# Both parts of the activation as one 512-column moving operand in the streamed products of a two-layer decoder trunk, one output per accumulator bank, weights split 1024 columns at a time

## The chip, the cores and the metric

The kernel runs on one core of one Trainium2 chip. The metric is the device time of one launch in microseconds (us). Three runs of the kernel before took 921.65, 922.49 and 922.83 us; the median is 922.49 us.

## The reference, cut to what matters

Sequence 256, width 1024, float32. Layer 0 mixes tokens by attention in three dilated groups, layer 1 by an mLSTM block. After each mixer come a squared-ReLU MLP and a gated embedding.

```
x += dilated_attention(rms_norm(x) ...) @ w_o          # layer 0, w_qkv 1024 x 9216
x += mlstm(rms_norm(x) @ w_up ...) @ w_down            # layer 1, w_up 1024 x 4096
x += square(relu(rms_norm(x) @ w1)) @ w2               # each layer, hidden 4096
x += sigmoid(rms_norm(x) @ w_gate) * (p @ w_proj)      # each layer
```

Features lie on the 128 partitions, tokens (256) along the free axis, so a product reads the weights as the stationary operand (128x128) and the activation as the moving one (256 columns per block of 128 features).

## The kernel before, in words

**Two parts.** Weights and activations are float32 and are multiplied as float32r. Each is split in two, a high part (ScalarE copy into float32r, L176 for weights, L298 for activations) and a low part (VectorE, value minus high part, L177 and L299). A product is hi*hi + hi*lo + lo*hi: three matmuls.

**The stream of weights.** All weights lie in units of 128 x 2048 (`UC`), 138 in all, loaded by SyncE four units ahead (`LD`). A unit is four slots of 512 columns; a slot is four weight tiles of 128x128. `open_slot` issues the split of slots up to `lead` ahead (7 in the qkv stage, 11 later), each into one of 12 buffers of 512 columns (`HU`) for either part. A split waits for the buffer, so for the matmuls that read it 12 slots before. The splits have a low priority (`BACK`): the scheduler puts them behind more urgent work in the queues.

**Stages, in order:** qkv with the attention between it (36 units; here the weights are the moving operand, 512 columns, L499 to L501), proj0 (1 unit), wo in two parts woA (k 0 to 5, 3 units) and woB (k 6 and 7, 1 unit), w1_0 (16), w2_0 (16), gate0 (4), xm (8), z0 to z3 (8) with the mLSTM core between them, wd0 (4), proj1 (1), wd1 (4), w1_1 (16), w2_1 (16), gate1 (4). From proj0 on, every product goes through `stream` (L318): per weight tile three matmuls of 256 columns, L331 (hi weights, high activation), L332 (hi weights, low activation), L333 (lo weights, high activation). Without the two proj stages that is 100 units, 1600 tiles.

**Accumulators.** `psa` has 3 buffers of one PSUM bank. Mostly a bank holds a pair of outputs o (2 x 256 columns); w2 and the end of woB, gate and wd1 have one output per bank. When all k of a block are done, `done` empties the bank: ReLU and square in w1 (L646 to L650), times the norm factor in w2 (L658), gate (L669), xm (L774) and z (L929), an addition to x in wo and wd (L623).

**Norm factors.** `rstd_rows` sums squares 2 slots after a stage's start (`SA`) and spreads the factor over the partitions 6 slots after it (`SB`): small VectorE operations, two scalings of the identity (L291), two matmuls (L293), a copy (L294, tile rb). In gate and xm the emptying of the first banks needs that factor and is put off by 3 slots (`DF`).

The order on each engine is set by a list scheduler from program order and priorities; queues are in order, so whoever waits holds up all behind it.

```
mm(acc[:, q], wh, h, start=first, stop=False, ...)   # L331
mm(acc[:, q], wh, l, start=False, stop=False, ...)   # L332
mm(acc[:, q], wl, h, start=False, stop=last, ...)    # L333
```

Of the kernel before, what the change touches and what calls it, by code (L numbers as in the profile page):

```python
# [14 lines left out]
ALU = mybir.AluOpType  # L15
# [14 lines left out]
HU = 512  # L30
# [9 lines left out]
def _blocks(no, ks, singles=0):  # L40

    n = no - singles
    os = [(o, o + 1) for o in range(0, n, 2)] + [(o,) for o in range(n, no)]
    return [(b, list(ks)) for b in os]

# [94 lines left out]
def _build(ctx, tc, nc, a):  # L140
# [17 lines left out]

    raw, hi, lo = {}, {}, {}
# [23 lines left out]
    CH = 512  # L183
    WARM = 9
    BACK = 100

    LQ, LS, LD = 7, 11, 4
    fill = {}
    clock = [0]
    ahead = [7]  # L190
# [6 lines left out]
    DF = 3  # L197
# [51 lines left out]
    hA = [base.tile([P, KT, S], F32R, name=f"h{n}") for n in "hl"]  # L249
# [68 lines left out]
    def stream(blocks, rhs, done, defer=0):  # L318

        i = 0  # L320
        for os, ks in blocks:
            n = len(os)
            acc = psa.tile([P, n, S], F32, name="acc")
            for k in ks:
                for q, o in enumerate(os):
# [3 lines left out]
                    h, l = rhs(k)  # L329
                    first, last = k == ks[0] and q == 0, k == ks[-1]  # L330
# [3 lines left out]
                    if last and q == n - 1:  # L334
                        if defer and i < 16:
                            at(clock[0] + defer, done, os, acc)
                        else:
                            done(os, acc)
# [4 lines left out]
    def from_h(h):  # L343
        return lambda k: (h[0][:, k], h[1][:, k])
# [79 lines left out]
    oT = [atp.tile([P, KT, S], F32R, name=f"oT{n}") for n in "hl"]  # L424
# [58 lines left out]
    def qkv_block(qt, what, g):  # L483
# [591 lines left out]
```

## Time and profile before

| | |
|---|---|
| median of three runs | 922.49 us |
| the profiled execution | 921.63 us, its span 919.9 us |
| TensorE (PE) busy | 904.3 us, 98% |
| VectorE (DVE) busy | 659.7 us, 72% |
| ScalarE (ACT) busy | 569.5 us, 62% |
| GpSimd (POOL) busy | 41.5 us, 5% |
| DMA | 150.23 MB, 163 GB/s mean |
| mean granted TensorE clock | 0.997 |

Busy time is the time in which an engine had at least one instruction in flight; matmuls and operations overlap their neighbours, so a pitch (start to start of neighbours that wait for nothing) is shorter than a duration. PEld is the weight load. A wait is put down to the instruction that released it. In the window view a matmul that is cut by an edge counts in both windows.

### The profile page before, as it was taken

The numbers are of one execution on the slowest core, as the hardware profiler recorded it, in microseconds if no ns is written. First come the engines' busy times: TensorE is split into PE (matmuls) and PEld (weight loads), VectorE is DVE, ScalarE is ACT, GpSimd is POOL, SyncE is SP. The second block draws the span as 40 slices with busy tenths as digits, with TensorE's granted clock in tenths as the row PEclk, the third lists the DMA queues.
The fourth block names the chain that finished last, engine by engine and source line by source line (L and its number), as shares of the span: only waits on it lengthen the run. The fifth ranks groups of instructions, "written<-read, shape, count | busy, mean of one in ns | idle before, by whom it ended". The sixth has DMA issues, their size and how long they took to land.

```text
span 919.9 us, 17609 instructions
## 1 busy us (share of the span) xinstructions
PE 904.3 (98%) x6924; PEld 844.3 (92%) x6924; DVE 659.7 (72%) x1409; ACT 569.5 (62%) x1055; POOL 41.5 (5%) x77
## 2 busy tenths in 40 slices
PE   8799999999999999999999999999999999999997
PEld 6687787877889999999999899999999999999997
DVE  6966877857866866665667987568898666656664
ACT  7567576575585766654446686668866666644442
POOL 0400000000000000000000542000000000000000
PEclk9999999999999999999999999999999999999999
DMA  8744443544443555555555433343265555555521
GB/s 302 281 142 160 156 144 133 178 136 145 154 161 105 178 185 183 184 183 184 183 184 183 157 129 104 127 138 98 87 220 204 184 183 184 184 183 182 184 94 46
DMA packets 23122, 150.23 MB, mean 163 GB/s; under 512 B 2560, under 2 KB 3200, under 8 KB 5632
## 3 DMA queue, kind: packets, MB, share of 16 engines
q1 hardware_dynamic: 23040, 149.12, 47.1%
q8 instruction: 54, 0.88, 0.4%
q14 instruction: 28, 0.23, 0.1%
HBM read 148.06 MB, written 1.05 MB: 162 GB/s over the span
## 4 chain that ended last, share of the span: by engine, by line
PE 92%; DVE 6%; ACT 1%; issue 1%; DMA 0%; SPq 0%; ACTq 0%
PE acc L331 21%; PE acc L332 21%; PE acc L333 21%; PE acc L499 6%; PE acc L501 6%; PE acc L500 6%; DVE lo L177 2%; PE tp L451 1%; PE tp L552 1%; PE sm L570 1%; PE sc L527 1%; PE tp L741 1%; PE tp L751 1%; PE sc L882 1%; PE sc L759 1%; PE sc L533 1%
## 5 line engine op out<-in xcount | busy, mean ns | idle before, releaser
L177 DVE TENSOR_TENSOR lo<-raw,hi 128x512 fp32r<-128x512 f32 x552 | 375.6, 691 | 176.7 <-ACT hi L176 175.3
L176 ACT ACTIVATE hi<-raw 128x512 fp32r<-128x512 f32 x552 | 339.2, 628 | 227.1 <-PE acc L332 204.4
L331 PE MATMUL acc<-hh,hi 128*128 128x256 f32 x640 | 184.0, 288 | 0.3 <-ACT hh L298 0.2
L332 PE MATMUL acc<-hl,hi 128*128 128x256 f32 x640 | 181.5, 284 | 0.1
L333 PE MATMUL acc<-hh,lo 128*128 128x256 f32 x640 | 181.4, 283 | 0.0
L331 PE MATMUL acc<-hidh,hi 128*128 128x256 f32 x512 | 144.9, 283 | 0.0
L332 PE MATMUL acc<-hidl,hi 128*128 128x256 f32 x512 | 144.9, 283 | 0.0
L333 PE MATMUL acc<-hidh,lo 128*128 128x256 f32 x512 | 144.9, 283 | 0.0
L331 PEld LDWEIGHTS acc<-hh,hi 128*128 128x128 f32 x640 | 122.4, 191 | 1.6 <-issue 0.7
L332 PEld LDWEIGHTS acc<-hl,hi 128*128 128x128 f32 x640 | 122.5, 191 | 0.7 <-DVE hl L299 0.5
L333 PEld LDWEIGHTS acc<-hh,lo 128*128 128x128 f32 x640 | 122.4, 191 | 0.0
L499 PE MATMUL acc<-hi,hh 128*128 128x512 f32 x264 | 109.6, 416 | 0.0
L500 PE MATMUL acc<-lo,hh 128*128 128x512 f32 x264 | 104.1, 394 | 0.8 <-DVE lo L177 0.8
L501 PE MATMUL acc<-hi,hl 128*128 128x512 f32 x264 | 104.2, 395 | 0.0
L331 PEld LDWEIGHTS acc<-hidh,hi 128*128 128x128 f32 x512 | 98.3, 192 | 0.0
L332 PEld LDWEIGHTS acc<-hidl,hi 128*128 128x128 f32 x512 | 98.3, 192 | 0.0
L333 PEld LDWEIGHTS acc<-hidh,lo 128*128 128x128 f32 x512 | 98.3, 192 | 0.0
L331 PE MATMUL acc<-hBh,hi 128*128 128x256 f32 x320 | 90.9, 284 | 0.0
L332 PE MATMUL acc<-hBl,hi 128*128 128x256 f32 x320 | 90.7, 283 | 0.0
L333 PE MATMUL acc<-hBh,lo 128*128 128x256 f32 x320 | 90.6, 283 | 0.0
L331 PEld LDWEIGHTS acc<-hBh,hi 128*128 128x128 f32 x320 | 61.4, 192 | 0.3 <-issue 0.3
L332 PEld LDWEIGHTS acc<-hBl,hi 128*128 128x128 f32 x320 | 61.4, 192 | 0.0
(258 smaller groups left out, 1384.3 us busy)
## 6 DMA issues: line engine op xcount, KB each, us to landing
raw<-w SPq DMA_DIRECT2D x136, 1024.0 KB, 4.9
raw<-w SPq DMA_DIRECT2D x8, 256.0 KB, 6.8
x<-x SPq DMA_DIRECT2D x4, 256.0 KB, 5.4
pj<-rep SPq DMA_DIRECT2D x1, 896.0 KB, 6.9
out<-u SPq DMA_DIRECT2D x3, 256.0 KB, 2.4
pT<-p SPq DMA_DIRECT2D x2, 256.0 KB, 4.0
nd<-nd SPq DMA_DIRECT2D x1, 384.0 KB, 6.2
out<-u SPq DMA_DIRECT2D x2, 128.0 KB, 1.9
```

Of the source, the lines that this page charges most:

```text
L176: act(hi[n][:, d], raw[u][:, s], AF.Copy)
L177: dve.tensor_tensor(lo[n][:, d], raw[u][:, s], hi[n][:, d], op=ALU.subtract)
L331: mm(acc[:, q], wh, h, start=first, stop=False, skip_group_check=n > 1)
L332: mm(acc[:, q], wh, l, start=False, stop=False, skip_group_check=n > 1)
L333: mm(acc[:, q], wl, h, start=False, stop=last, skip_group_check=n > 1)
L451: nc.tensor.transpose(ps[:, pair, b * P:(b + 1) * P], n[:, b, ty * 256 + pair * P:ty * 256 + (pair + 1) * P], ident)
L499: mm(accs[b], hh, wh, start=(k == 0), stop=False)
L500: mm(accs[b], hh, wl, start=False, stop=False)
L501: mm(accs[b], hl, wh, start=False, stop=(k == 7))
L527: mm(ps[:, 0:256], q[r, pair, tb], k[r, pair], start=first, stop=last)
L533: mm(ps[64 * e:64 * e + 64, 256 + 64 * n:320 + 64 * n], QT[qt, g][0][r, pair, t4], KTt[qt, g][0][r, pair, t4], start=True, stop=True)
L552: nc.tensor.transpose(psf[:, k * P:(k + 1) * P], pe[:, k * P:(k + 1) * P], ident)
```

## The change

Each activation is one tile with both parts behind each other ([P, 2, k, 256]), and a matmul with the hi weights takes both parts of one k as one moving operand of 2 x 256 columns (the two runs lie KT x 256 or, in the MLP, 32 x 256 elements apart). Its result fills a whole bank: one half has hi*hi, the other hi*lo; the lo*hi matmul adds into the first half. So a tile has two matmuls, 512 and 256 columns, and a bank holds one output. Whoever empties it adds the halves: `whole`, a ScalarE copy of one half and a VectorE addition of the other, or two additions to x. The proj stages keep the old form (`stream_pairs`). A split covers 1024 columns, two slots, into one of 6 buffers; the leads are 6 and 10. In gate and xm the bank is emptied at once and the rest of the work waits for the factor (`late`). A stage begins with two outputs side by side, the others follow one by one (w2 and z: all one by one). The input of proj shares its tiles with others (tags).

```diff
-HU = 512
+HU = 1024
-def _blocks(no, ks, singles=0):
-    n = no - singles
-    os = [(o, o + 1) for o in range(0, n, 2)] + [(o,) for o in range(n, no)]
+def _blocks(no, ks, first=2):
+    os = [tuple(range(first))] + [(o,) for o in range(first, no)]
...
-        with tc.high_priority(offset=-(BACK if back is None else back)):
-            act(hi[n][:, d], raw[u][:, s], AF.Copy)
-            dve.tensor_tensor(lo[n][:, d], raw[u][:, s], hi[n][:, d], op=ALU.subtract)
+        s = slice(c * 512, (c + n) * 512)
+        d = slice(c * 512 % HU, c * 512 % HU + n * 512)
+        with tc.high_priority(offset=-back):
+            act(hi[t][:, d], raw[u][:, s], AF.Copy)
+            dve.tensor_tensor(lo[t][:, d], raw[u][:, s], hi[t][:, d], op=ALU.subtract)
+    def parts(p, name, *shape, **k):
+        t = p.tile([P, 2, *shape], F32R, name=name, **k)
+        return [t, t[:, 0], t[:, 1]]
-    LQ, LS, LD = 7, 11, 4
+    LQ, LS, LD = 6, 10, 4
-        while ahead[0] < clock[0] + lead[0]:
-            ahead[0] += 1
+        while ahead[0] + 2 <= clock[0] + lead[0]:
+            ahead[0] += 2
             split(*divmod(ahead[0], 4))
...
-    def stream(blocks, rhs, done, defer=0):
+    def stream(blocks, h, done):
-            acc = psa.tile([P, n, S], F32, name="acc")
+            accs = [psa.tile([P, 2, S], F32, name="acc") for _ in os]
...
-                    mm(acc[:, q], wh, h, start=first, stop=False, skip_group_check=n > 1)
-                    mm(acc[:, q], wh, l, start=False, stop=False, skip_group_check=n > 1)
-                    mm(acc[:, q], wl, h, start=False, stop=last, skip_group_check=n > 1)
+                    mm(acc.rearrange("p a b -> p (a b)"), wh, h[0][:, :, k], start=first, stop=False, skip_group_check=True)
+                    mm(acc[:, 0], wl, h[1][:, k], start=False, stop=last, skip_group_check=True)
+                    if last:
+                        done(o, acc)
...
+    def late(t0, f, *args):
+        if clock[0] > t0 + SB:
+            f(*args)
+        else:
+            at(t0 + SB, f, *args)
+    def whole(out, acc):
+        act(out, acc[:, 1], AF.Copy)
+        dve.tensor_tensor(out, out, acc[:, 0], op=ALU.add)
...
-    prep, ph = proj(0, atp, ("n0", "n1", "sqh"))
+    prep, ph = proj(0, atp, ("sqh", "nqk"))
...
-            dve.tensor_tensor(x[:, span(os)], x[:, span(os)], acc, op=ALU.add)
+            for n in range(2):
+                dve.tensor_tensor(x[:, o], x[:, o], acc[:, n], op=ALU.add)
...
-            act(u, acc, AF.Relu)
-            dve.tensor_tensor(s, u, u, op=ALU.mult)
-            act(hid[0][:, span(os)], u, AF.Square)
-            dve.tensor_tensor(hid[1][:, span(os)], s, hid[0][:, span(os)], op=ALU.subtract)
+            whole(u[:, o % 2], acc)
+            if o % 2:
+                dve.scalar_tensor_tensor(s, u, 0.0, u, op0=ALU.max, op1=ALU.mult)
+                act(hid[1][:, o - 1:o + 1], s, AF.Copy)
+                dve.tensor_tensor(hid[2][:, o - 1:o + 1], s, hid[1][:, o - 1:o + 1], op=ALU.subtract)
...
-            dve.tensor_tensor(t, acc[:, 0], r2, op=ALU.mult)
+            whole(t, acc)
+            dve.tensor_tensor(t, t, r2, op=ALU.mult)
...
+        def rest(o, t):
+            dve.tensor_tensor(t, t, rb, op=ALU.mult)
+            act(g, t, AF.Sigmoid)
+            dve.tensor_tensor(t, g, pj[:, o], op=ALU.mult)
+            finish(o, t)
+        def done(o, acc):
+            t = tmp.tile([P, S], F32, name="gt", bufs=3)
+            whole(t, acc)
+            late(t0, rest, o, t)
-        stream(B_GATE, from_h(h2), done, DF)
+        stream(B_GATE, h2, done)
...
-        dve.tensor_tensor(xm, acc, urb[0][:, None, :].to_broadcast([P, 2, S]), op=ALU.mult)
+        whole(xm[:, o % 2], acc)
+        late(xm0, xm_rest, o - 1, xm)
+    def xm_rest(o, xm):
+        dve.tensor_tensor(xm, xm, urb[0][:, None, :].to_broadcast([P, 2, S]), op=ALU.mult)
...
-            dve.tensor_tensor(t, acc, urb[0][:, None, :].to_broadcast([P, 2, S]), op=ALU.mult)
-            act(sz[:, span(os)], t, AF.Silu)
+            whole(t[:, o % 2], acc)
+            if o % 2:
+                dve.tensor_tensor(t, t, urb[0][:, None, :].to_broadcast([P, 2, S]), op=ALU.mult)
+                act(sz[:, o - 1:o + 1], t, AF.Silu)
```

TensorE in w1_0, before (acc is the bank, hh and hl the parts of the activation, hi and lo those of the weights):

```order
L331 MATMUL acc<-hh,hi 128x256
L332 MATMUL acc<-hl,hi 128x256
L333 MATMUL acc<-hh,lo 128x256
L331 MATMUL acc<-hh,hi 128x256
L332 MATMUL acc<-hl,hi 128x256
L333 MATMUL acc<-hh,lo 128x256
```

And now (h is the activation with both parts):

```order
L338 MATMUL acc<-h,hi 128x512
L339 MATMUL acc<-h,lo 128x256
L338 MATMUL acc<-h,hi 128x512
L339 MATMUL acc<-h,lo 128x256
L338 MATMUL acc<-h,hi 128x512
L339 MATMUL acc<-h,lo 128x256
```

Three matmuls and three weight loads of a tile have become two of each.

VectorE in gate0 from the first operation that needs the factor rb, before (u is the emptied pair of outputs, s its sigmoid, xn the next layer's input, hl and hh its parts):

```order
L669 TENSOR_TENSOR u_6020<-acc_5877,rb_5876 128x512
L669 TENSOR_TENSOR u_6049<-acc_5949,rb_5876 128x512
L177 TENSOR_TENSOR lo_6065<-raw_5882,hi_6064 128x512
L672 TENSOR_TENSOR u_6020<-s_6022,pj_198 128x512
L672 TENSOR_TENSOR u_6049<-s_6051,pj_198 128x512
L697 TENSOR_TENSOR xn_5870<-x_82,u_6020 128x4x4x16 x2
L697 TENSOR_TENSOR xn_5870<-x_82,u_6049 128x4x4x16
L299 SCALAR_TENSOR_TENSOR hl_116<-xn_5870,prm_83,hh_115 128x256 x2
L697 TENSOR_TENSOR xn_5870<-x_82,u_6049 128x4x4x16
L177 TENSOR_TENSOR lo_6083<-raw_5954,hi_6082 128x512
```

And now (gt is one emptied output; L376 is the addition of the halves):

```order
L704 TENSOR_TENSOR gt_4852<-gt_4852,rb_4804 128x256
L704 TENSOR_TENSOR gt_4857<-gt_4857,rb_4804 128x256
L704 TENSOR_TENSOR gt_4883<-gt_4883,rb_4804 128x256
L707 TENSOR_TENSOR gt_4852<-s_4920,pj_189 128x256
L707 TENSOR_TENSOR gt_4857<-s_4927,pj_189 128x256
L738 TENSOR_TENSOR xn_4799<-x_82,gt_4852 128x4x4x16
L738 TENSOR_TENSOR xn_4799<-x_82,gt_4857 128x4x4x16
L182 TENSOR_TENSOR lo_4998<-raw_4865,hi_4997 128x1024
L306 SCALAR_TENSOR_TENSOR h_115<-xn_4799,prm_83,h_115 128x256 x2
L707 TENSOR_TENSOR gt_4883<-s_4936,pj_189 128x256
L376 TENSOR_TENSOR gt_4950<-gt_4950,acc_4886 128x256
L738 TENSOR_TENSOR xn_4799<-x_82,gt_4883 128x4x4x16
```

The chain works on one output at a time; the emptying of the fourth output's bank (acc_4886) stands inside it, behind a split of 1024 columns.

ScalarE at the end of gate1, before:

```order
L294 ACTIVATE rb_11025<-sm_11077 128x256
L671 ACT_TABLE_LOAD
L671 ACTIVATE s_11159<-u_11157 128x512
L671 ACTIVATE s_11178<-u_11176 128x512
L671 ACTIVATE s_11234<-u_11232 128x512
L671 ACTIVATE s_11266<-u_11264 128x256
L671 ACTIVATE s_11298<-u_11296 128x256
```

And now, its last ten:

```order
L375 ACTIVATE gt_8856<-acc_8801 128x256
L375 ACTIVATE gt_8882<-acc_8865 128x256
L375 ACTIVATE gt_8908<-acc_8891 128x256
L706 ACTIVATE s_8860<-gt_8856 128x256
L706 ACTIVATE s_8886<-gt_8882 128x256
L706 ACTIVATE s_8912<-gt_8908 128x256
L375 ACTIVATE gt_8934<-acc_8917 128x256
L375 ACTIVATE gt_8960<-acc_8943 128x256
L706 ACTIVATE s_8938<-gt_8934 128x256
L706 ACTIVATE s_8964<-gt_8960 128x256
```

The copy of the last output's half (acc_8943) stands ahead of the last two sigmoids.

## Rows read from the trace of the kernel before

**Rows 1.** The page: busy time, and the chain that ended last, by engine
```profile
PE 904.3 (98%) x6924; PEld 844.3 (92%) x6924; DVE 659.7 (72%) x1409; ACT 569.5 (62%) x1055; POOL 41.5 (5%) x77
...
PE 92%; DVE 6%; ACT 1%; issue 1%; DMA 0%; SPq 0%; ACTq 0%
```

**Rows 2.** Windows: start:end, length, busy and instructions per engine, PEclk, DMA
```profile
20.00:40.00 20.00, 19.11 (x91) 15.06 (x89) 19.69 (x51) 13.26 (x26) 4.84 (x7) 1.00 0.72 263
40.00:60.00 20.00, 14.92 (x65) 12.17 (x66) 14.24 (x34) 8.86 (x18) 7.82 (x15) 0.91 0.56 191
...
300.00:320.00 20.00, 19.90 (x167) 19.73 (x166) 18.05 (x37) 14.60 (x29) 0.00 (x0) 1.00 0.55 197
340.00:360.00 20.00, 20.00 (x169) 20.00 (x169) 13.70 (x22) 11.87 (x20) 0.00 (x0) 1.00 0.60 202
500.00:520.00 20.00, 19.65 (x160) 19.05 (x160) 18.71 (x38) 16.49 (x31) 4.58 (x3) 1.00 0.34 116
520.00:540.00 20.00, 18.74 (x141) 17.64 (x141) 19.37 (x44) 14.08 (x26) 13.07 (x24) 1.00 0.49 164
...
640.00:660.00 20.00, 20.00 (x157) 19.11 (x156) 16.52 (x50) 14.92 (x26) 0.00 (x0) 1.00 0.38 134
660.00:680.00 20.00, 20.00 (x166) 19.85 (x166) 19.38 (x47) 14.39 (x29) 0.00 (x0) 1.00 0.48 170
```

**Rows 3.** Timeline of TensorE in qkv: start, duration, line, tiles
```profile
62.13 0.39 PE L499 MATMUL acc<-hi,hh 128*128 128x512 f32 x1
...
66.89 0.39 PE L499 MATMUL acc<-hi,hh 128*128 128x512 f32 x1
```

**Rows 4.** Timeline of TensorE in w1_0
```profile
344.87 0.28 PE L332 MATMUL acc<-hl,hi 128*128 128x256 f32 x1
...
349.91 0.28 PE L332 MATMUL acc<-hl,hi 128*128 128x256 f32 x1
```

**Rows 5.** Groups by line and shape: busy us, mean ns, idle before
```profile
L177 DVE TENSOR_TENSOR lo<-raw,hi 128x512 fp32r<-128x512 f32 x552 | 375.6, 691 | 176.7 <-ACT hi L176 175.3
L658 DVE TENSOR_TENSOR u<-acc,rb 128x256 f32<-128x256 f32 x16 | 6.8, 425 | 2.4 <-PE acc L333 0.4
```

**Rows 6.** Timeline of VectorE in w1_0: five splits in a row
```profile
311.35 3.09 DVE L177 TENSOR_TENSOR lo<-raw,hi 128x512 fp32r<-128x512 f32 x5
```

**Rows 7.** Timeline of VectorE at the end of w2_0
```profile
487.97 0.43 DVE L659 TENSOR_TENSOR x<-x,u 128x256 f32<-128x256 f32 x1
488.31 0.68 DVE L177 TENSOR_TENSOR lo<-raw,hi 128x512 fp32r<-128x512 f32 x1
```

**Rows 8.** Who waited for whom: total us, times, longest
```profile
PE tp L451 <- DVE nqk L443: 5.2, 2, 5.0
...
PE sm L293 <- DVE dg L291: 1.3, 1, 1.3
```

**Rows 9.** Timeline of TensorE after its longest wait, in qkv
```profile
44.89 0.45 PE L451 MATMUL tp<-ident,nqk 128*128 128x128 f32 x1 [5.02 <-DVE nqk L443]
...
45.56 0.63 PE L500 MATMUL acc<-lo,hh 128*128 128x512 f32 x1
45.98 0.63 PE L501 MATMUL acc<-hi,hl 128*128 128x512 f32 x1
```

**Rows 10.** Timeline in gate0, all engines: the factor rb
```profile
498.51 0.37 ACT L294 ACTIVATE rb<-sm 128x256 f32<-128x256 f32 x1
```

**Rows 11.** Timeline of VectorE at the start of xm
```profile
517.30 0.52 DVE L299 SCALAR_TENSOR_TENSOR hl<-xn,prm,hh 128x256 fp32r<-128x256 f32 x1
```

**Rows 12.** Timeline at the end, after the last matmul
```profile
915.23 0.42 DVE L669 TENSOR_TENSOR u<-acc,rb 128x256 f32<-128x256 f32 x1 [1.02 <-PE acc L333]
915.75 0.42 ACT L671 ACTIVATE s<-u 128x256 f32<-128x256 f32 x1 [2.46 <-DVE u L669]
916.20 0.43 DVE L672 TENSOR_TENSOR u<-s,pj 128x256 f32<-128x256 f32 x1 [0.54 <-ACT s L671]
916.66 0.42 DVE L978 TENSOR_TENSOR u<-xn,u 128x256 f32<-128x256 f32 x1
```

More of the change, by code (lines that the diff above doesn't have):

```diff
@@ L29, with _pairs @@
 UC = 2048
-HU = 512
+HU = 1024
 SC = 384
 PI = np.array([16 * c + 4 * b + a for a in range(4) for b in range(4) for c in range(16)])
-def _blocks(no, ks, singles=0):
-    n = no - singles
-    os = [(o, o + 1) for o in range(0, n, 2)] + [(o,) for o in range(n, no)]
+def _blocks(no, ks, first=2):
+    os = [tuple(range(first))] + [(o,) for o in range(first, no)]
     return [(b, list(ks)) for b in os]
+def _pairs(no, ks):
+    return [((o, o + 1), list(ks)) for o in range(0, no, 2)]
 def _qkv():
@@ L247, in pr @@
         return prm[:, o:o + w]
-    hA = [base.tile([P, KT, S], F32R, name=f"h{n}") for n in "hl"]
+    hA = parts(base, "h", KT, S)
     sqp = pool("sq", 2)
@@ L328, in stream @@
                     wh, wl = weights(u, (i % 16) * P, P)
[L329 to L338 removed]
+                    acc, first, last = accs[q], k == ks[0], k == ks[-1]
+                    mm(acc.rearrange("p a b -> p (a b)"), wh, h[0][:, :, k], start=first, stop=False, skip_group_check=True)
+                    mm(acc[:, 0], wl, h[1][:, k], start=False, stop=last, skip_group_check=True)
+                    if last:
+                        done(o, acc)
                     if i % 4 == 3:
@@ L341, in stream, with stream_pairs @@
                     i += 1
-    def from_h(h):
-        return lambda k: (h[0][:, k], h[1][:, k])
+    def stream_pairs(blocks, h, done):
+        i = 0
+        for os, ks in blocks:
+            acc = psa.tile([P, 2, S], F32, name="acc")
+            for k in ks:
+                for q, o in enumerate(os):
+                    if i % 4 == 0:
+                        u, c = open_slot()
+                    wh, wl = weights(u, (i % 16) * P, P)
+                    first, last = k == ks[0] and q == 0, k == ks[-1]
+                    mm(acc[:, q], wh, h[1][:, k], start=first, stop=False, skip_group_check=True)
+                    mm(acc[:, q], wh, h[2][:, k], start=False, stop=False, skip_group_check=True)
+                    mm(acc[:, q], wl, h[1][:, k], start=False, stop=last, skip_group_check=True)
+                    if last and q == 1:
+                        done(os, acc)
+                    if i % 4 == 3:
+                        close_slot()
+                    i += 1
+    def late(t0, f, *args):
[6 more added lines that the diff above has]
+        dve.tensor_tensor(out, out, acc[:, 0], op=ALU.add)
     actx = ExitStack()
@@ L422, in _build @@
     at(44, small_products)
-    oT = [atp.tile([P, KT, S], F32R, name=f"oT{n}") for n in "hl"]
+    oT = parts(atp, "oT", KT, S)
     QT, KTt, VT = {}, {}, {}
@@ L602, in proj @@
         nc.sync.dma_start(ptile, a["p"][layer])
-        ph = [p.tile([P, 2, S], F32R, name=f"pT{n}", tag=tags[n]) for n in (1, 2)]
+        ph = parts(p, "pTp", 2, S, tag=tags[1])
         def prep():
-            act(ph[0], ptile, AF.Copy)
-            dve.tensor_tensor(ph[1], ptile, ph[0], op=ALU.subtract)
+            act(ph[1], ptile, AF.Copy)
+            dve.tensor_tensor(ph[2], ptile, ph[1], op=ALU.subtract)
         return prep, ph
-    prep, ph = proj(0, atp, ("n0", "n1", "sqh"))
+    prep, ph = proj(0, atp, ("sqh", "nqk"))
     prep()
@@ L676, in _build @@
     mctx = ExitStack()
     mp = pool("mlp0", c=mctx)
-    hid = [mp.tile([P, 32, S], F32R, name=f"hid{n}") for n in "hl"]
+    hid = parts(mp, "hid", 32, S)
     hgp = pool("hG", c=xctx0, side="right")
-    hG = [hgp.tile([P, KT, S], F32R, name=f"hG{n}") for n in "hl"]
+    hG = parts(hgp, "hG", KT, S)
     gst = Stats()
@@ L687, in _build @@
     xn = xp1.tile([P, KT, S], F32, name="xn")
-    hB = [xp1.tile([P, KT, S], F32R, name=f"hB{n}") for n in "hl"]
+    hB = parts(xp1, "hB", KT, S)
     mctx = ExitStack()
@@ L876, in memory @@
         nums = []
+        sq = zp.tile([P, 2, 512], F32, name="nsq")
         ss = None
@@ L972, in _build, with finish1 @@
     mp = pool("mlp1", c=mctx)
-    hid = [mp.tile([P, 32, S], F32R, name=f"hid{n}") for n in "hl"]
+    hid = parts(mp, "hid", 32, S)
     gst = Stats()
     mlp(1, x, hB, mst, hid, mp, hA, "gP1", gst)
-    def finish1(os, t):
-        dve.tensor_tensor(t, x[:, span(os)], t, op=ALU.add)
-        nc.sync.dma_start(a["out"][:, span(os)], t)
+    def finish1(o, t):
+        dve.tensor_tensor(t, x[:, o], t, op=ALU.add)
+        nc.sync.dma_start(a["out"][:, o], t)
     gate(1, hA, gst, mp, finish1)
```

148 lines of the change are left out of this document (73 added, 75 removed).

## The prediction

> **What bounds the kernel now.** I read the page first. TensorE is busy for 98% of the span and 92% of the chain that ended last is its own work [rows 1]. An edit gains what it takes from TensorE's queue and loses every wait that it puts into it; work on VectorE and ScalarE counts only through such waits. Next come the windows [rows 2]: in w1_0 (340:360) TensorE has no idle time and does 169 matmuls in 20 us at full clock. VectorE has 6 us to spare there, but only 2.0 in woB (300:320), 1.3 where gate0 goes into xm (500:520), and 0.6 in xm's first part (520:540) and in wd0 (660:680). The list of waits holds one long wait of TensorE, 5.0 us, and one of 1.3 us for a factor's diagonals [rows 8].
>
> Last, the timeline for the two pitches. From 62.13 to 66.89 lie 21 matmuls of 512 columns: 4.76/21 = 226.7 ns each [rows 3]. From 344.87 to 349.91 lie 42 of 256: 5.04/42 = 120.0 ns [rows 4]. At the higher level (2.4 GHz) the columns themselves take 213.3 and 106.7 ns, so a matmul pays 13.3 ns beside its columns at either width.
>
> **Term 1, the matmuls.** A tile had three matmuls, 3 x 120.0 = 360.0 ns. It will have one of 512 and one of 256: 226.7 + 120.0 = 346.7 ns. Columns and results are the same; one fixed cost of 13.3 ns goes. 100 units of 16 tiles give 1600 x 13.3 ns = 21.3 us. All of it lies on TensorE, thus on the path: **-21.3 us**. What the rows don't show is a moving operand in two runs, far apart: those of both rows are contiguous. Bounds: the jump is free (-21.3), or a second run pays what a matmul pays, 13.3 ns (0). I take free: the fixed part is the same at both widths, so it goes with the instruction and not with the columns read.
>
> The Trainium skill's page "TensorE: Matmul & The Clock Gate", section "Wait — 56ns, not 53.3ns?", gives about 2.5 ns beside the columns, 215.7 ns at 512. By it 1600 x 2.5 = 4 us go (an estimate from that page). The rows of this kernel disagree with it: 226.7 and 120.0 ns.
>
> **Term 2, the split of weights.** Two splits of 512 become one of 1024. Five in a row on VectorE take 3.09 us [rows 6], the last one's duration being 0.69 [rows 5]; the pitch is (3.09 - 0.69)/4 = 0.60 us, and that of 256 columns is 488.31 - 487.97 = 0.34 [rows 7], so 256 columns more take 0.26. A wide split then costs between 0.60 + 2 x 0.26 = 1.12 us and 2 x 0.60 = 1.20; I take 1.12. It frees VectorE of 0.08 us per pair of slots, but an urgent operation behind it waits up to 1.12 us instead of 0.60.
>
> The page "Perfetto Trace Analysis" of the Trainium skill, section "Optimizing Scalar/DVE Operations", speaks for and against: larger operations help an engine that is saturated, but where one that isn't causes bubbles elsewhere, breaking up instructions may let work end sooner. No row of before has a 1024-wide split.
>
> Where it decides: at the start. VectorE is busy 19.69 of 20 us from 20 to 40 [rows 2], and TensorE then waits 5.0 us until 44.89 for nqk, whose operations stand behind splits; then its matmuls come at 45.98 - 45.56 = 0.42 us, the lower level (1.2 GHz), and the window has a mean clock of 0.91 [rows 2, 8, 9]. Some 20 splits stand ahead of nqk: 20 x 0.60 - 10 x 1.12 = 0.8 us less of work, and half as many places at which a chain of small operations can be parted by a split. Bounds: 0, where the longer operations take it back, and -6, where the wait goes entirely and with it about 1 us of lost clock (40:60). Nearest to the first by work alone; I take **-2.0**.
>
> **Term 3, emptying the banks.** One operation with two outputs becomes, per output, a copy on ScalarE and an addition on VectorE. The copy is priced by that of 256 columns out of PSUM, 0.37 us [rows 10]; the addition by L658, also out of PSUM: 0.425 long [rows 5], pitch 0.34 [rows 7]. Three banks now hold three outputs, not six. An output of eight k takes 8 x 0.347 = 2.8 us on TensorE, so a bank may be emptied up to 5.5 us late, against 11.5 before. In w1, w2, w_down's second half and woA this hides: VectorE has 6 us of 20 free (340:360) [rows 2] and by the prices above, each output needs at most 2 x 0.34 us more there, in 2.8 us or more. Nothing there. Where it need not hide:
>
> woB: an output has two k, 0.69 us on TensorE; VectorE has two additions (0.68), a low part (0.4, between the 0.34 of a pitch and the 0.52 of its own row [rows 11]) and a share in a sum of squares, with 2.0 us free in 20 [rows 2]. Eight outputs need some 8 x 1.3 = 10 us against 5.5 us of TensorE; three banks and the next stage's first tiles, which need the first parts only, cover all but **+1.5** (0 to 4).
>
> gate0 into xm: the factor rb is done at 498.88 [rows 10], and the last part of xm's input, k = 7, at 517.82 [rows 11]: 18.9 us of VectorE in a row. The change adds five additions there (1.7), breaks pairs into single outputs (0.5), widens the splits between (5 x 1.12 - 7 x 0.60 = 1.4), and 0.6 us of idle time can go: 21.9. On TensorE the spread of the factor now stands behind 35 of the gate's 64 tiles (12.1 us), so rb lands some 13.0 us after the gate's start; the gate ends at 64 x 0.347 = 22.2, and in the new order 22 tiles of xm (of three outputs, 7.6) stand ahead of the first k = 7: 29.8, or 16.8 behind rb. VectorE is late by 21.9 - 16.8 = 5.1 us. The wait for xm's own factor, behind the same queue, adds about 1.0. Before, TensorE lost 9 matmuls here against w1_0 (160 against 169, 1.1 us) and the 1.3 us for the diagonals [rows 2, 8], and these go: 6.1 - 2.4, some **+3.5** (0 to 7).
>
> xm's first part: 0.6 us of VectorE are free in 20, TensorE is 1.3 short of full [rows 2]; **+0.5** (0 to 2).
>
> The mLSTM core (z, wd0): the change adds 2 x 0.34 - 0.14 = 0.54 us of VectorE per unit, seven units in 40 us, to 16.52 + 19.38 = 35.9 us [rows 2]: 39.7 in the 38.5 us that TensorE now needs. The splits' lead of 10 slots (13.9 us of TensorE) takes up most: **+1.5** (0 to 10).
>
> gate1: fourth and later outputs wait for the third gt buffer, so for a DMA out; **+1.0** (0 to 3). The tail: from 915.23 to 917.08 is 1.85 us [rows 12]. In the new order the copy and addition (0.8) stand ahead, and the last two sigmoids behind them (0.42 more): **+1.2** (0.8 to 1.6).
>
> **Sum.** -21.3 - 2.0 + 1.5 + 3.5 + 0.5 + 1.5 + 1.0 + 1.2 = -14.1. Against the profiled execution, 921.63 us: 907.5. The median of the runs shown is 0.86 above that execution; the forecast is 908.4 us.
>
> **The rivals.**
>
> (b) The stalls hide and the start gains. Term 3 then comes to about +2 (the tail and one spread), term 2 to -5: 922.5 - 21.3 - 5 + 2 = 898 (895 to 903). For it: all banks but a few are emptied without delay before, and PE is busy without a gap over whole stages [rows 2]. Against it: the windows where VectorE has under 2 us left.
>
> (c) VectorE takes over as the bound from gate0 to wd0. If no lead covers it, the core costs +10 instead of 1.5 and xm +2 instead of 0.5: 918 (913 to 921). For it: 19.37 and 19.38 of 20 [rows 2]. Against it: between these windows VectorE drops to 16.52, and TensorE lost little there.
>
> (d) Slower: each run of the moving operand pays the fixed 13.3 ns, as a matmul of 256 columns does. The saving is 0, and the terms 2 and 3 cost 9.2 - 2.0 = 7.2 us: 922.5 + 7.2 = 930. It decides from (21.3 - 7.2)/1600 = 8.8 ns per tile up. For it: nothing shows a jump for free. Against it: the equal fixed part at both widths, above.
>
> (e) Slower by less: a run pays four fifths of the 13.3 ns, so that 2.7 ns a tile are saved, 1600 x 2.7 = 4.3 us: 922.5 - 4.3 + 7.2 = 925. For and against it stands what stands for (d). The Trainium skill's 2.5 ns, above, come to nearly the same time; the rows speak against them.
>
> That the change doesn't do what it says is excluded by the order of instructions: two matmuls per tile in all 100 units.
>
> **How the numbers follow.** Forecast 0.55, (b) 0.22, (c) 0.15, (d) 0.05, (e) 0.03. What a measurement can tell from no change is 0.2%, 1.8 us. Faster are the first two and nearly all of (c), 0.13 of 0.15: 0.90; the rest of (c) is the same, 0.02; slower are (d) and (e), 0.08. The likeliest's own range is 903 to 913. The range goes from the middle of (b), 898, to the middle of (c), 918, and leaves out about 2 in 10.
>
> **What would show it.** Term 1: in w1_0, L338 and L339 come at 226.7 and 120.0 ns, a pair every 346.7; a pair at 360 is (d). Term 2: L182 at 1024 columns about 1.2 us long, and the wait for nqk shorter than 5.0. Term 3: w1 and w2 without a gap; waits of TensorE ahead of xm's first k = 7 of about 5 us, and for the factors; in the core VectorE nearly full without long waits of TensorE, while waits of over 5 us there mean (c). At the end 3.1 us from the last matmul's result to the last operation. A stage of w1 that has gaps would make the forecast wrong, as would a pitch over 355 ns.

## The result and the profile after

The changed kernel takes 931.06 us (median of 4 runs, 930.6 to 931.9), the kernel before 922.51 in the same comparison: 1.0095 times as long, 95% interval 1.0078 to 1.0113. It is slower, by 8.6 us; forecast were 908.4, 898 to 918. The profiled execution took 931.13 us, its span is 929.4 (before 919.9).

The page of the changed kernel, busy time, two groups and the chain that ended last; they answer to [rows 1, 5]:

```profile
PE 902.3 (97%) x5324; PEld 761.9 (82%) x5324; DVE 684.4 (74%) x1326; ACT 544.1 (59%) x884; POOL 37.6 (4%) x77
L182 DVE TENSOR_TENSOR lo<-raw,hi 128x1024 fp32r<-128x1024 f32 (+1 forms) x280 | 338.9, 1213 | 176.9 <-ACT hi L181 175.2
L376 DVE TENSOR_TENSOR u<-u,acc 128x256 f32<-128x256 f32 x80 | 33.1, 414 | 0.5 <-ACT u L375 0.3
PE 86%; DVE 9%; ACT 2%; DMA 2%; issue 1%; SPq 0%; ACTq 0%
```

TensorE's share of the chain fell from 92% to 86%, VectorE's rose from 6 to 9: work has been taken from TensorE and waits put in. The windows of [rows 2] in the changed kernel (same columns), and two of 5 us:

```profile
20.00:40.00 20.00, 17.36 (x79) 13.64 (x78) 18.17 (x37) 11.88 (x15) 1.42 (x3) 1.00 0.72 269
40.00:60.00 20.00, 16.55 (x69) 12.92 (x67) 13.19 (x32) 7.04 (x11) 10.36 (x19) 0.83 0.39 132
300.00:320.00 20.00, 18.51 (x108) 15.79 (x107) 19.18 (x43) 13.77 (x24) 0.00 (x0) 1.00 0.31 106
340.00:360.00 20.00, 20.00 (x115) 17.33 (x114) 15.59 (x22) 10.96 (x18) 0.00 (x0) 1.00 0.54 197
520.00:540.00 20.00, 18.00 (x99) 15.20 (x98) 18.56 (x40) 11.30 (x21) 9.15 (x18) 0.91 0.50 176
640.00:660.00 20.00, 15.92 (x91) 13.26 (x90) 18.91 (x47) 13.59 (x23) 0.00 (x0) 0.96 0.45 158
...
655.00:660.00 5.00, 1.39 (x6) 1.09 (x7) 4.98 (x10) 2.33 (x3) 0.00 (x0) 0.83 0.13 52
660.00:665.00 5.00, 4.18 (x13) 3.25 (x12) 4.26 (x19) 3.67 (x10) 0.00 (x0) 0.50 0.71 219
```

w1_0 (340:360) is still without a gap. New is what happens after 655: TensorE works 1.39 of 5 us, VectorE 4.98, and then the granted clock is 0.50, the lower level, for five us. The list of TensorE's waits in the changed kernel (total, times, longest) gives the cause, and answers to [rows 8]:

```profile
PE tp L483 <- DVE nqk L475: 4.6, 4, 3.1
PE acc L338 <- DVE hB L975: 4.4, 2, 3.6
PE acc L338 <- DVE gt L376: 2.6, 2, 1.9
PE acc L338 <- DVE h L306: 2.0, 1, 2.0
PE acc L532 <- DVE lo L182: 1.5, 1, 1.5
PE acc L338 <- DVE x L656: 1.5, 2, 1.3
```

hB is the input of wd0, made by VectorE at the end of a head's chain in the mLSTM core; gt an output in gate0 whose bank must be emptied; h the input of xm; x the one of w1_0. None of these four lines was there before. The other two belong to qkv: the longest wait for nqk fell from 5.0 to 3.1 us, and that for the low part of a split (lo) was 0.8 us before.

To see where the 9.5 us of span come from, take the start of each stage's first matmul in the two timelines. Lengths in us:

| | before | after | difference |
|---|---|---|---|
| start to woA | 270.3 | 272.2 | +2.0 |
| woA, woB | 31.7 | 33.9 | +2.2 |
| w1_0, w2_0, w1_1, w2_1 | 370.5 | 363.4 | -7.1 |
| gate0 | 23.9 | 26.0 | +2.1 |
| xm to proj1 | 171.7 | 180.3 | +8.7 |
| wd1 | 23.0 | 22.2 | -0.8 |
| gate1 | 24.1 | 25.1 | +1.1 |
| behind the last matmul | 4.7 | 6.1 | +1.4 |

Two things differ from the forecast. The MLP gains 7.1 us, not 1024 x 13.3 ns = 13.6; and the core loses 8.7 net of what its tiles gain. The pitch of a tile of w1_0 in the changed kernel's timeline (from the first row to the last are 27 tiles):

```profile
340.21 0.40 PE L338 MATMUL acc<-h,hi 128*128 128x512 f32 x1
...
349.75 0.40 PE L338 MATMUL acc<-h,hi 128*128 128x512 f32 x1
```

9.54/27 = 353.3 ns, where [rows 3, 4] had given 226.7 + 120.0 = 346.7: half of the 13.3 ns are saved. But in wd1 of the same execution, with the same two matmuls, 27 tiles take 9.36 us, 346.7 ns each:

```profile
699.76 0.39 PE L338 MATMUL acc<-h,hi 128*128 128x512 f32 x1
...
709.12 0.39 PE L338 MATMUL acc<-h,hi 128*128 128x512 f32 x1
```

So there are two pitches, and both stand in one execution. By the start times in the trace, the step from a matmul of 512 columns to the next one of 256 takes 236.7 ns on average in w2_0 and 230.2 in wd1; the step back takes 116.7 in both.

VectorE in the core of the changed kernel, head 1, from its first small operation (dd) to hB (start, duration, line, tiles):

```profile
641.98 0.16 DVE L954 SCALAR_TENSOR_TENSOR dd<-sm,em 128x2 f32<-128x2 f32 x1 [1.07 <-PE sm L952]
642.06 1.22 DVE L182 TENSOR_TENSOR lo<-raw,hi 128x1024 fp32r<-128x1024 f32 x1
643.19 0.15 DVE L955 TENSOR_TENSOR dd<-sm,dd 128x2 f32<-128x2 f32 x1
...
643.92 1.22 DVE L182 TENSOR_TENSOR lo<-raw,hi 128x1024 fp32r<-128x1024 f32 x1
645.06 0.17 DVE L288 TENSOR_SCALAR ff<-vv 128x2 int32<-128x2 int32 x1
645.13 1.22 DVE L182 TENSOR_TENSOR lo<-raw,hi 128x1024 fp32r<-128x1024 f32 x1
646.26 0.42 DVE L376 TENSOR_TENSOR zt<-zt,acc 128x256 f32<-128x256 f32 x1
646.59 0.16 DVE L290 TENSOR_TENSOR rt<-ff 128x2 f32<-128x2 f32 x1
...
658.30 0.69 DVE L975 TENSOR_TENSOR hB<-mt,hB 128x512 fp32r<-128x512 f32 x1
```

An operation of 0.15 us that the next one needs stands behind a split of 1.22 us, or behind an addition, again and again. From dd to hB pass 16.3 us, and six wide splits stand between them. Before, the same chain took 14.5 us, with nine narrow ones:

```profile
635.04 0.16 DVE L901 SCALAR_TENSOR_TENSOR dd<-sm,em 128x2 f32<-128x2 f32 x1 [0.52 <-PE sm L899]
...
649.52 0.69 DVE L922 TENSOR_TENSOR hBl<-mt,hBh 128x512 fp32r<-128x512 f32 x1
```

### The profile page after: what moved, and what is told of

It is laid out like the page before. It is cut to its first block, busy times and chain, and to the rows that moved or that the text cites. A ratio compares the mean times of both kernels' runs of the same rounds, so it can differ in the third digit from the quotient of the medians.

```text
span 929.4 us, 13889 instructions
## 1 busy us (share of the span) xinstructions
PE 902.3 (97%) x5324; PEld 761.9 (82%) x5324; DVE 684.4 (74%) x1326; ACT 544.1 (59%) x884; POOL 37.6 (4%) x77
## 4 chain that ended last, share of the span: by engine, by line
PE 86%; DVE 9%; ACT 2%; DMA 2%; issue 1%; SPq 0%; ACTq 0%
PE acc L338 37%; PE acc L339 19%; PE acc L531 6%; PE acc L533 6%; PE acc L532 6%; DVE lo L182 3%; PE tp L483 1%; PE tp L584 1%; PE sm L602 1%; ACT hi L181 1%; PE sc L559 1%; DVE y L832 1%; DMA raw<-w 1%; PE sc L565 1%; PE sc L935 1%
## 5 line engine op out<-in xcount | busy, mean ns | idle before, releaser
L182 DVE TENSOR_TENSOR lo<-raw,hi 128x1024 fp32r<-128x1024 f32 (+1 forms) x280 | 338.9, 1213 | 176.9 <-ACT hi L181 175.2
L181 ACT ACTIVATE hi<-raw 128x1024 fp32r<-128x1024 f32 (+1 forms) x280 | 291.9, 1046 | 233.1 <-PE acc L338 144.2
L338 PE MATMUL acc<-h,hi 128*128 128x512 f32 x640 | 230.5, 402 | 3.1 <-DVE h L306 2.0
L339 PE MATMUL acc<-h,lo 128*128 128x256 f32 x640 | 181.3, 284 | 0.0
L338 PE MATMUL acc<-hid,hi 128*128 128x512 f32 x512 | 181.0, 399 | 0.0
L338 PEld LDWEIGHTS acc<-h,hi 128*128 128x128 f32 x640 | 120.9, 189 | 32.9 <-DVE h L306 2.9
L339 PE MATMUL acc<-hid,lo 128*128 128x256 f32 x512 | 143.8, 281 | 0.0
L339 PEld LDWEIGHTS acc<-h,lo 128*128 128x128 f32 x640 | 121.6, 190 | 0.3
L338 PE MATMUL acc<-hB,hi 128*128 128x512 f32 x320 | 115.4, 404 | 4.4 <-DVE hB L975 4.4
L338 PEld LDWEIGHTS acc<-hid,hi 128*128 128x128 f32 x512 | 96.2, 188 | 23.9
L531 PE MATMUL acc<-hi,h 128*128 128x512 f32 x264 | 110.0, 418 | 0.0
L533 PE MATMUL acc<-hi,h 128*128 128x512 f32 x264 | 104.5, 396 | 0.0
L376 DVE TENSOR_TENSOR u<-u,acc 128x256 f32<-128x256 f32 x80 | 33.1, 414 | 0.5 <-ACT u L375 0.3
L574 ACT ACTIVATE scs<-scs,m 128x384 f32<-128x384 f32 x32 | 19.5, 610 | 22.4 <-DVE m L573 21.9
```

Of the source, the lines that this page charges most:

```text
L181: act(hi[t][:, d], raw[u][:, s], AF.Copy)
L182: dve.tensor_tensor(lo[t][:, d], raw[u][:, s], hi[t][:, d], op=ALU.subtract)
L338: mm(acc.rearrange("p a b -> p (a b)"), wh, h[0][:, :, k], start=first, stop=False, skip_group_check=True)
L339: mm(acc[:, 0], wl, h[1][:, k], start=False, stop=last, skip_group_check=True)
L376: dve.tensor_tensor(out, out, acc[:, 0], op=ALU.add)
L531: mm(accs[b], hh, wh, start=(k == 0), stop=False)
```

## The experiments

Theories: P, the emptying by two operations and one output per bank is what makes the tight stages slow; W, the splits of 1024 columns; J, a jump in the moving operand costs the missing 6.7 ns per tile. The ratios below are to the kernel before in the same comparison.

### 1. Both parts contiguous

```diff
-        t = p.tile([P, 2, *shape], F32R, name=name, **k)
-        return [t, t[:, 0], t[:, 1]]
+        t = p.tile([P, shape[0], 2, shape[1]], F32R, name=name, **k)
+        return [t, t[:, :, 0], t[:, :, 1]]
```

> The changed kernel with one thing different: both parts of one k lie next to each other ([P, k, 2, 256]), so that the 512 columns of the moving operand are one contiguous run. In the changed kernel a tile takes 353.3 ns where the forecast had 346.7. Theory J (the jump between the two runs costs 6.7 ns): a pair of matmuls now every 346.7 ns in the MLP, 1600 x 6.7 = 10.7 us less, 920 us (919 to 923, since stalls in the core may grow by what TensorE gains). Rival R (the 6.7 ns come from neighbours of different width, a weight load hidden behind 256 columns only): the pitch stays at 353 and the time at 930 to 932.

928.79 us, 1.0074 (1.0058 to 1.0091). J is refuted: in w1_0 the same 27 tiles take 9.54 us. But in w2_1, where the changed kernel's profile has 353 ns, stands (28 tiles):

```profile
820.21 0.39 PE L338 MATMUL acc<-hid,hi 128*128 128x512 f32 x1
...
829.91 0.39 PE L338 MATMUL acc<-hid,hi 128*128 128x512 f32 x1
```

9.70/28 = 346.4 ns: layer 0 has one pitch and layer 1 the other, with one layout throughout, as the changed kernel has both (w1_0 and wd1) with the other layout. So neither J nor a fixed cost of the change of width (R) describes it.

### 2 and 3. Narrow splits in the changed kernel, wide ones in the kernel before

```diff
-HU = 1024
+HU = 512
-    LQ, LS, LD = 6, 10, 4
+    LQ, LS, LD = 7, 11, 4
```

> The changed kernel with splits of 512 columns, 12 buffers and leads of 7 and 11 slots, as before the change; all else as changed. Theory P (the waits in gate0, xm and wd0 come from the added additions and from one output per bank): the waits before xm's first k = 7 and for hB in wd0 remain within 1 us, only the start gets back its 2 us: 928 to 930. Rival W (they come from urgent operations that stand behind splits of 1.2 us): the wait of 3.6 us for hB and the low clock behind it go, 2.0 us at the start, some 6 in wd0, 2 in gate0: 920 to 923.

917.18 us, 0.9931 (0.9906 to 0.9957). The longest wait for hB falls to 1.8 us, xm to proj1 takes 173.1 us instead of 180.3; the start 270.2.

```profile
PE acc L338 <- DVE hB L975: 1.8, 1, 1.8
```

The stages go W's way (wd0 and proj1 37.6 us instead of 41.9, the wait for xm's input 0.7 instead of 2.0) except gate0 (25.4 instead of 26.0, where W had 2 us), but the time lies below both ranges. W's does not hold the 3.1 us that layer 1's MLP gains here because its tiles come at 346.7 ns, which has nothing to do with the splits (runs 8 and 9).

The reverse edit, in the kernel before:

```diff
-HU = 512
+HU = 1024
-    LQ, LS, LD = 7, 11, 4
+    LQ, LS, LD = 6, 10, 4
```

> The kernel before with the change's splits alone: 1024 columns, 6 buffers, leads 6 and 10; the matmuls and the emptying of banks as before. Theory P: only the start is later by about 2 us and at most 1 us is lost in the core: 923 to 926. Rival W: the wait for hB in wd0 is there too, with the low clock behind it: 929 to 933.

920.89 us, 0.998 (0.997 to 0.999): wide splits alone are a gain. Neither theory had that. The start is not later (270.4) and xm to proj1 takes 170.0, not 171.7; head 1's chain from dd to hB is 12.4 us long here, against 14.5, with three wide splits in it. wo is 1.0 us longer than before.

### 4 and 5. The old form in the tight stages, with wide and with narrow splits

woB, both gates, xm, z and wd0 again with `_old` blocks (two outputs to a bank) and three matmuls of 256, emptied by one operation; woA, w1, w2 and wd1 as changed.

```diff
-        stream(B_Z, hA, done)
+        stream_pairs(B_Z, hA, done)
```

> The changed kernel with the old form (three matmuls of 256 columns, two outputs per bank, one operation to empty it) in woB, gate0, xm, z, wd0 and gate1, and the new one in woA, w1, w2 and wd1; splits of 1024 columns as changed. Theory P: the losses of the changed kernel in these stages go (2.6 in wo, 2.5 in gate0, 2.7 in xm and z, 8 in wd0, 1.5 in gate1, 1.4 at the end, 18.7 us in all) and 464 tiles x 6.7 ns = 3.1 us of the saving go with them: 915.5 (914 to 919). Rival W: what stands behind wide splits still waits, 5 us or more of TensorE's waits in wd0 stay: 922 to 928.

912.69 us, 0.9894 (0.988 to 0.9909), better than P said: 3.1 us are again layer 1's MLP at 346.7 ns, 2.1 the start. The wait for hB is gone; gate0 24.5, xm to proj1 170.9, behind the last matmul 4.7.

With the edit of run 2 on top:

> The kernel of the run with the old form in the tight stages (woB, gate0, xm, z, wd0, gate1), now with splits of 512 columns, 12 buffers, leads 7 and 11. Theory M (wide splits hurt only where additions fill VectorE as well; without them their 0.08 us per pair of slots is a gain, as in the kernel before with wide splits alone): about 2 us slower than with wide splits, 914 to 916. Rival W (a wide split always delays what stands behind it): 1 to 3 us faster, 910 to 912.

914.3 us, 0.99 (0.9872 to 0.9929), too near the one before to tell by time alone, with executions from 911.3 to 916.4; its profiled one has 353.3 ns in both layers, 3.2 us that the profiled one of run 4 doesn't pay. By stages: xm to proj1 171.7 against 170.9, but wo 32.1 against 33.1, where a wait of 0.9 us for x is gone. So M in the core, W in wo. The four corners for xm to proj1, in us:

| | splits of 512 | splits of 1024 |
|---|---|---|
| old form | 171.7 (before; also run 5) | 170.0 (run 3), 170.9 (run 4) |
| new form | 173.1 (run 2) | 180.3 (after) |

Alone, the new form costs 1.4 us and the wide splits gain 1.7; together they cost 8.7. The loss needs both: P and W each had half of the cause. Head 1's chain shows the same: 14.5 us before, 12.4 with wide splits alone, 14.3 with the new form alone, 16.3 with both.

### 6 and 7. Which stage's new form

The old form in woB, the gates and xm, the new one in z and wd0:

```diff
-    stream(B_XM, hA, xm_done)
+    stream_pairs(B_XM, hA, xm_done, DF)
```

> The changed kernel with the old form in woB, gate0, gate1 and xm; z and wd0 keep the new one, splits of 1024. Theory E (the core is late because xm already started late, by its wait for the input and the low clock behind it): the wait for hB in wd0 falls below 1 us, wd0 and proj1 together take 35 to 36.5 us, 914 to 916. Rival C (the additions of z, in the chain from a head's factor to hB, make it late): the wait for hB stays at 2.5 us or more with low clock behind it, wd0 and proj1 take 39 us or more, 918 to 921.

917.9 us, 0.9948 (0.9933 to 0.9963). Rival C holds: xm takes 69.7 us instead of 73.2, yet wd0 and proj1 take 42.9, head 1's chain 16.3, and the list of waits has the same line as the changed kernel's:

```profile
PE acc L345 <- DVE hB L977: 4.4, 2, 3.6
```

So the late start of xm has no part in the wait for hB. All four MLP stages of this profile have the pitch of 346.7 ns.

And the old form in z alone:

```diff
-B_Z = _blocks(4, range(8), 1)
+B_Z = _old(4, range(8))
```

> The changed kernel with the old form in z alone (one operation empties a bank of two outputs); gate0, xm, wd0 and all else as changed. Theory C (z's copies and additions delay the chain from a head's factor to hB): the wait for hB goes, below 1 us, and proj1 begins sooner, wd0 and proj1 together 35 to 37 us in place of 41.9: 924 to 926. Rival D (wd0's own double additions and the late start of xm are as much to blame): 39 us or more there, 928 to 931.

919.63 us, 0.9967 (0.9954 to 0.998), lower than expected by some 5 us, of which the start (268.5 instead of 272.2) and the pitch in layer 1 (346.7 ns, below) have nothing to do with z. The wait for hB is gone, wd0 and proj1 take 34.2 us instead of 41.9, and head 1's chain 12.4 instead of 16.3, with three wide splits in it instead of six: 3.6 us of splits instead of 7.3, nearly all of the difference. TensorE in that stretch works without a gap (windows of run 7):

```profile
640.00:650.00 10.00, 10.00 (x76) 9.30 (x75) 9.15 (x28) 7.51 (x11) 0.00 (x0) 1.00 0.54 169
650.00:660.00 10.00, 10.00 (x63) 8.54 (x62) 8.95 (x25) 8.77 (x10) 0.00 (x0) 1.00 0.24 75
```

But xm and z together are 3.2 us longer (141.5 against 138.4). Half of it is z, whose tiles have three matmuls again, half is xm, 74.7 us against 73.2: the wait for its input is 2.0 us in both, but the granted clock from 520 to 540 is 0.83 here and 0.91 there. And xm to proj1 is 175.7, where run 4 has 170.9: xm itself takes 74.7 us against 69.7 in runs 4 and 6, which have the old form in gate0 and xm. How much of these 5.0 us is the wait and the clock behind it, and how much xm's own emptying, no run separates. The chain that ends in hB is thus made late by z's new form, less by the time of its additions than by the splits that then stand in the chain; the core as a whole loses by that and by xm.

### 8 and 9. The two pitches

One tiny matmul behind every 16 tiles of w2:

```diff
+                    if tick and i % tick == 0:
+                        tt = pst.tile([P, 2, S], F32, name="tp")
+                        mm(tt[:, 0, 0:1], ones, ones[:, 0:1], start=True, stop=True)
```

> The kernel with the old form in the tight stages, with one tiny matmul (128x1, its result is not used) behind every 16 tiles of w2, 32 in all. Rival S (a phase that any interruption sets anew): in both layers' w2 the pitch between two of them changes among 346.7, 350.0 and 353.3 ns from stretch to stretch. Theory L (set by something that differs between the layers, as the place of their tiles): 353.3 ns in all stretches of w2_0, 346.7 in all of w2_1. Each tiny matmul costs 0.05 to 0.3 us in either case, 914 to 922.

921.63 us (one execution). In layer 0 the scheduler put all sixteen ahead, into woB, and two of layer 1's into wd1, so only the fourteen in w2_1 answer. There, on TensorE (the first six):

```profile
814.33 0.28 PE L354 MATMUL tp<-ones 128*128 128x1 f32 x2
820.20 0.28 PE L354 MATMUL tp<-ones 128*128 128x1 f32 x2
825.98 0.28 PE L354 MATMUL tp<-ones 128*128 128x1 f32 x2
831.85 0.28 PE L354 MATMUL tp<-ones 128*128 128x1 f32 x2
837.73 0.28 PE L354 MATMUL tp<-ones 128*128 128x1 f32 x2
843.50 0.28 PE L354 MATMUL tp<-ones 128*128 128x1 f32 x2
```

The stretches of 16 tiles take 5.87, 5.78, 5.87, 5.88, 5.77 us. The short ones are shorter by 0.10 us, which is 16 x 6.7 ns = 0.107. Between two tiny matmuls the tiles come at 353 or at 347 ns: S holds, in that the pitch changes at such an interruption and stays until the next one. In this run every third stretch is a short one.

The changed kernel once more, without an edit:

> The changed kernel once more. Theory S (a phase, set anew by interruptions, that can differ from execution to execution): its profile may show 346.7 ns a tile in one layer, then 3.4 us less, and the executions fall 3 us or so apart. Rival F (fixed by the program): 353.3 ns in both layers again, 930 to 932. At the start, wo begins at 270.2 as in the other kernels with the same splits if the 2 us there were chance, at 272.2 if not.

929.56 us, 1.0074 (1.0045 to 1.0102); its executions are 926.3, 927.7, 931.5 and 931.9. In the profiled one (927.66) layer 0 has 353.3 ns, layer 1 has 346.7 (28 tiles in w2_1):

```profile
820.08 0.39 PE L338 MATMUL acc<-hid,hi 128*128 128x512 f32 x1
...
829.78 0.39 PE L338 MATMUL acc<-hid,hi 128*128 128x512 f32 x1
```

So the same program runs in either state. Of the eight profiles of runs with this order in both layers of the MLP and nothing put in between, two have 353.3 ns in both layers (the changed kernel's first and run 5), one has 346.7 in both (run 6), and five have 353.3 in layer 0 and 346.7 in layer 1. One layer's MLP in the better one is worth 512 x 6.7 ns = 3.4 us. The start was 271.2 us here, between the two values expected.

### 10 to 12. Another order of the matmuls, and the parts put together

To the kernel of run 4:

```diff
-                    mm(acc[:, 0], wl, h[1][:, k], start=False, stop=last, skip_group_check=True)
+                    two.append((o, k, acc, wl, last))
+                    if i % 2:
+                        for o_, k_, a_, w_, l_ in two:
+                            mm(a_[:, 0], w_, h[1][:, k_], start=False, stop=l_, skip_group_check=True)
```

> The kernel with the old form in the tight stages, but in the new form the matmuls of two tiles stand as 512, 512, 256, 256 in place of 512, 256, 512, 256. In the runs so far a tile of the MLP takes either 353.3 ns (layer 0) or 346.7 (layer 1, except in the changed kernel), whatever the layout of the moving operand. Theory T (the 6.7 ns are paid where a 512 follows a 256): half as many such places, 350.0 ns in layer 0, 512 x 3.3 = 1.7 us less: 911 (910 to 912). Rival S (it is a phase of TensorE's stream that any interruption sets anew): the pitch is again one of a few fixed values, constant over a stage, no matter how many such places there are, and the time within 2 us of 912.7.

910.95 us, 0.9867 (0.9851 to 0.9883). w2_0 and w2_1 both take 89.17 us, 348.3 ns a tile, where 353.3 would be 90.45 and 346.7 be 88.75. It is neither of the two old values, and the same in both layers: the time lies where both theories had it, the pitch where neither did.

To that, with woA in the old form as well:

```diff
+            if 38 <= v <= 44:
+                split(v, d, 1)
+                split(v, d + 1, 1)
+            else:
+                split(v, d)
```

> Put together: the new form in w1, w2 and wd1 alone, with the order 512, 512, 256, 256; the old form elsewhere, woA too; splits of 1024 columns, each as two of 512 while wo runs (units 38 to 44). From the run with that order (910.95): wo 1.0 us shorter by the narrow splits and woA within 0.3 us either way: 909.9 (908 to 911.5). If narrow splits do nothing in wo: 911.

909.15 us, 0.9854 (0.9839 to 0.9868), as expected: wo 31.5 us instead of 32.9, by both edits together. This version beats both kernels, by 1.5% the one before; its gain is the MLP's and wd1's. TensorE is back at 90% of the chain (its page):

```profile
PE 893.4 (98%) x5836; PEld 782.8 (86%) x5836; DVE 659.8 (73%) x1242; ACT 531.6 (59%) x845; POOL 37.5 (4%) x77
...
PE 90%; DVE 6%; DMA 1%; ACT 1%; issue 1%; SPq 0%; ACTq 0%
```

And four by four:

```diff
-                    if i % 2:
+                    if i % 4 == 3:
```

> The same with four matmuls of 512 columns and then four of 256. That order of two and two took 348.3 ns a tile, 1.7 above the 346.7 that two fixed parts leave. Theory T (3.3 ns for each place where a 512 follows a 256): 0.83 ns a tile less, 347.5, 1088 tiles: 0.9 us faster than with two and two, 909. Rival S (one of a few fixed values whatever the number of such places): equal within 0.5 us, or off by 1.7 ns x 1088 = 1.8 us either way.

911.55 us, 0.9882 (0.9866 to 0.9899): w2 takes 89.81 us in both layers, 350.8 ns a tile, slower than two and two. Theory T (3.3 ns for each place where a 512 follows a 256) falls, and a few fixed values (S) no longer describe it either. The pitch depends on the pattern, in a way that these runs don't explain.

## Why the prediction was wrong, point by point

**Term 1, mis-sized.** -21.3 us were 1600 tiles x 13.3 ns. In the profiled execution a tile gained 6.7 ns in both MLPs: 1600 x 6.7 = 10.7 us, if all tiles are counted so. The step that failed is "226.7 + 120.0 = 346.7": two pitches, each from a stretch of like matmuls, were added for a stream that alternates between them. The stream has at least two steady states, 346.7 and 353.3 ns, and this execution had the dearer one in both layers, the cheaper one in wd0 and wd1. Where the sum comes out right (all MLP stages of run 6), its parts don't: the steps are 230.0 and 116.7 ns, not 226.7 and 120.0. What sets the state is open. The forecast's doubt was at the wrong place: the jump between the two runs costs nothing (run 1), so rivals (d) and (e) came near the time (930 and 925) by a mechanism that run 1 refutes; that is luck. The forecast's own signs of being wrong were too wide: a pitch over 355 ns and waits of over 5 us in the core did not appear.

**Term 3, the core: the place of rival (c).** +1.5 was taken, 0 to 10 given; measured are 8.7 net, and with the 320 tiles' gain (at least 320 x 6.7 ns = 2.1 us) 10.8. The step that failed is "the lead takes up most". VectorE's sum of work was the measure, and that was met (18.91 of 20 us). But the wait is not for a split, which the lead covers; it is for the end of a chain of small dependent operations, into which splits and additions are placed (16.3 us with six wide splits, 12.4 with three in run 7). Besides, the loss was counted without the clock: behind the wait of 3.6 us the granted clock was 0.50 (1.2 GHz) from 660 to 665, which takes up to 2.5 us more, and in the window of xm's wait its mean was 0.91, 9% of 20 us or 1.8 us. No term had that price for the new waits, though the window 40:60 of [rows 2] shows such a case.

**gate0 into xm, right in its mechanism.** From rb to the last part of the input the forecast had 21.9 us; in the changed kernel rb ends at 502.03, the part for k = 7 at 523.67: 21.6. The wait was 2.0 there, and 1.9 in gate0 for the fourth output's bank, which the sum did not have: 3.9 for 5.1 forecast.

**woB, gate1 and the tail.** wo lost 2.2 us net, 2.6 with its tiles' gain, for +1.5 (0 to 4). gate1 lost 1.1 net, 1.5 with that gain, for +1.0. From the last matmul to the end of VectorE's last operation it was 1.1 us longer than before, for +1.2.

**Term 2, right in the wait and wrong in the time.** A wide split takes 1.13 to 1.14 us (643.92 to 645.06, 645.13 to 646.26), as taken. The longest wait for nqk did fall: it is 5.0 us wherever the splits are narrow (before, runs 2 and 5) and 3.0 or 3.1 in all others. But the start is no sooner for it: woA begins at 270.1 to 270.4 in runs 1 to 4, with wide or narrow splits, as before. The step that failed is to take the gain in one wait for a gain of the stage. In run 3 the first of qkv's three matmul lines is 0.9 us ahead of the kernel before at its 41st matmul (44.1 against 45.0), 0.3 at its 81st and not at all at its 201st (184.2 in both). One place is the wait for a split's low part, which grew from 0.8 to 1.5 us; the others are not resolved. The changed kernel begins woA at 272.2, with 4.6 us of waits for nqk, run 9 at 271.2, with 3.6. Both have a granted clock of 0.83 from 40 to 60, where it is 0.91 before and in runs 1 to 4, and 1.00 in run 7, which has the same splits and begins woA at 268.5; run 5, also at 0.83, begins it at 270.9. So the start goes largely with the clock; why that differs among these executions is not shown.

What a wide split does elsewhere depends on the queue: from xm to proj1 narrow ones gain 7.2 us in the new form (run 2), wide ones 1.7 in the old one (run 3); in wo narrow ones are better by 0.7 to 1.0 us in each pair of kernels (runs 2, 3 and 5). The Trainium skill's page "Perfetto Trace Analysis", section "Optimizing Scalar/DVE Operations", lets saturation decide: larger operations where the engine is saturated, broken up ones where it isn't but causes bubbles elsewhere. Here breaking up paid (runs 2 and 5) though VectorE was busy for 18.91 of 20 us from 640 to 660 in the changed kernel and 18.24 from 300 to 320 in run 4, so the busy share alone did not decide.

**Sum.** Forecast -14.1, measured +9.5 in the span, 23.6 apart: 10.6 from term 1, 7.8 from gate0 to proj1 (13.3 with the tiles' gain, 2.5 in gate0 and 10.8 behind it, for 5.5), 4.0 from the start, 1.1 from wo, 0.7 from gate1 and the end, -0.6 from the rest. Every tile is counted with a gain of 6.7 ns here; most of those of wd0 and all of wd1 gained 13.3, which puts 0.4 us more into the core's loss and is most of the rest. The first two are shown by experiments, but not why a stream has one pitch or the other; the start is explained in part only.

## What to carry to other kernels

A pitch that was measured in a stretch of like matmuls is not the pitch of a stream that mixes two widths: give it a range, and let no forecast rest on the last 2% of it. A wait that gets shorter is not yet a stage that gets shorter. Where an engine is full, ask what chain of small dependent operations runs through its queue, and count how many long operations can stand between two of its links; two edits that cost 1.4 us and gain 1.7 alone cost 8.7 us together here. Price a new wait of some us with the lower clock that may follow it, and use a new form where the other engines have room (the MLP), not everywhere.

## What the runs showed of the hardware

The same 512 and 256 column matmuls came at 346.7 or 353.3 ns a pair, steady over hundreds of tiles; 350.0 was seen in short stretches of gate0. The difference lies in the step from the 512 to the 256: 236.7 ns in w2_1 of the changed kernel, 230.0 in run 9, with 116.7 for the step back in both. A tiny matmul in between can move the stream from one to the other, two executions of one program differ, and one execution can hold both. In the kernel before, with 256 columns throughout, no second value showed (w2_0 and w2_1 both 92.16 us). What the state is, is open.

In the order 512, 512, 256, 256 a tile took 348.3 ns, in groups of four 350.8, each the same in both layers. Nothing here says why.
